# The down-projection's banks evicted one by one, with the activation table, a held product and the tail's sums and multiplies moved

## The chip, the cores and the metric

The kernel runs on one core of one Trainium2 chip. The time of a run is the device time in microseconds (us). Shown are the median of three timed runs of the kernel before, and one further execution that the hardware profiler recorded; all rows of the trace are from that one.

The core has TensorE (PE, matmuls; PEld are its weight loads), VectorE (DVE), ScalarE (ACT), GpSimd (POOL) and SyncE (SP), which issues most of the transfers. SBUF holds the operands, and PSUM holds eight banks of 128 x 512 fp32 into which PE adds.

## The reference, cut to what matters

One layer: a token mixer with a residual, then a gated MLP with a residual, then a last norm. The change is in the last two lines.

```python
h = modulate(rmsnorm(x), sh2, sc2)
up = conv(h @ w_up) + conv_b              # (1024 tokens, 2 * 2816)
a, b = split(up)
x = x + g2 * ((silu(a) * b) @ w_down)     # w_down: 2816 x 1024
return rmsnorm(x) * final_norm            # x * rsqrt(mean(x*x) + eps) * final_norm
```

Everything is fp32: 1024 tokens, 1024 channels, 22 blocks of 128 hidden channels.

## The kernel before

Tensors lie transposed: channels on the 128 partitions, tokens along the row. `hf` is a half of the tokens (512) and `d` one of eight channel tiles; `xs[hf][d]` is a 128 x 512 tile of the residual stream, and the final result.

**The down-projection as seven products.** Hidden blocks, channels and tokens are each cut in two, and the 2 x 2 block product is made from seven products instead of eight, in the order 1, then 2 with 5, then 6 with 3 (interleaved), then 7, then 4 (list `steps`). A product has NJ = 11 steps; a step (p, j) multiplies one 128 x 512 block of activations with a 128 x 512 block of weights into four banks, one for each channel tile. A product of fp32 accuracy is three matmuls of a high and a low part (`mm3`, L107), so a step is 12 matmuls of 512 columns; the high part is a cast on ACT (L801), the low part a subtraction on DVE (L802). Sums and differences of blocks that the seven products need are made by DVE (L812). Products 1, 2, 6, 7 and 4 use one set of four banks and add on top of what stands there; 5 and 3 use another set. Product 4 adds onto product 7, so that PE may write a bank for product 4 only after DVE has read product 7 from it.

**Loads.** `prepare_d(n + 3)` keeps the operands three steps ahead: SP loads blocks (`da`, four buffers; `ra`, `rb`, `rb2` stay), then come the cast and the subtraction. A `da` buffer is reloaded when DVE has split what was in it.

**Evictions.** After the last step of a product, the loop at the end of the kernel treats the four banks: `evac` (L1110, DVE) computes xs = bank * gate + xs; products 1 and 5 are copied to `hold` tiles (ACT, L1212, L1215); product 1's copies are put back into the banks after product 2 is out (L1218); product 5's copies are added into the second half when product 7 ends. `squares` squares an xs tile on ACT (L1134) and adds it into `acc[hf]` on GpSimd (L1142).

**Norm and output.** `finish_first`, called after step (7, 3), sums `acc[0]` over the partitions with a matmul against ones (`ss`), makes rstd = exp(-0.5 * ln(...)) with two ACT instructions (L1146, L1147), and multiplies: `outputs` handles eight channel tiles, two to one store. Seven tiles are one DVE instruction (L1160: xs * gain * rstd), the eighth is ACT (times gain, L1157) and GpSimd (times rstd, L1158). Stores go alternately from SP and from ACT (L1162). The last step (4, 10) is cut in two halves of 256 tokens. `finish_last` sends, behind each half's matmuls, one `ss` matmul of `acc[1]`; at the very end come four more `ss` matmuls per half, one for each new square, and `outputs` again.

**The activation table.** `exp_ln` (L182) orders a table load for Ln and Exp (L184) behind a given ACT instruction: here behind the last Silu of the up-projection (L993).

**What sets the order.** PE runs in the order in which the code is written. The other engines' streams are ordered when the kernel is built, by what each instruction needs and where it stands in the code; each engine then runs its own stream strictly in order and waits on semaphores. GpSimd's last work of the up-projection is the store of a gated block (`gd`, L997), an addition (L1004) and its store (L1005).

## Time and profile before

| what | us |
|---|---|
| median of three timed runs | 1050.42 (1049.86 to 1051.85) |
| the profiled execution's own time | 1047.94 |
| its span | 1046.2 |
| PE busy | 1001.2 |
| DVE busy | 854.6 |
| ACT busy | 549.2 |
| GpSimd busy | 190.5 |

Times in rows are us from the start of the span. A timeline row is: start, duration, engine, line of the kernel, operation, output<-inputs, shape and count; in brackets the idle time of the engine before it and what ended that. Several like instructions in a row are merged, and then the duration runs from the first one's start to the last one's end. A row of the chain of waits is: start, duration, what the end was waiting for at that time. A row of waits is: who waited for whom, total, times, longest. A row of windows is: stretch, its length, then busy time and count of PE, PEld, DVE, ACT and POOL, then the clock granted to PE (1.00 is full), the busy share of the DMA engines and GB/s. PE rows of 512 columns are drawn with an overlap: twelve take 2.72 from start to next start. The letter q (SPq, ACTq) marks an engine's issuing of transfers.

### The profile page before, as it was taken

How to read it: one execution, taken by the hardware profiler on the slowest of the kernel's cores; microseconds unless marked ns; L12 is line 12 of the kernel's file. 1: busy time of each engine (PE TensorE's matmuls, PEld its weight loads, DVE VectorE, ACT ScalarE, POOL GpSimd, SP SyncE). 2: the span in 40 equal slices, each digit the busy share in tenths (PEclk: the TensorE clock that was granted, in tenths of full speed). 3: DMA queues.
4: the chain of work that ended last, by engine and by line, in shares of the span. 5: the costliest groups of instructions: out<-in, count | busy, mean ns of one | idle time of the engine just before them, and what ended most of it. 6: DMA issues, size and time to landing. Idle time of an engine off the chain costs nothing.

```text
span 1046.2 us, 12684 instructions
## 1 busy us (share of the span) xinstructions
PE 1001.2 (96%) x4481; PEld 815.4 (78%) x4481; DVE 854.6 (82%) x1197; ACT 549.2 (52%) x888; POOL 190.5 (18%) x163
## 2 busy tenths in 40 slices
PE   7989999998999989999999999999999999999995
PEld 5768868886777768877888888888888788888874
DVE  7967899689988849999977788777776776988883
ACT  5465585442733547665555455555554544644442
POOL 3437203222141030011100101101001000200210
PEclk8999999999999999999999999999999999999998
DMA  8743232455487442233222222332334787223642
GB/s 315 258 151 111 81 110 83 149 174 182 149 280 262 155 167 81 86 137 129 105 99 91 105 102 107 131 111 101 111 111 151 272 283 240 101 81 111 201 141 81
DMA packets 60817, 154.21 MB, mean 147 GB/s; under 512 B 6641, under 2 KB 9809, under 8 KB 60754
## 3 DMA queue, kind: packets, MB, share of 16 engines
q1 hardware_dynamic: 54192, 134.00, 37.8%
q0 software_dynamic: 4928, 17.30, 4.3%
q10 hardware_dynamic: 1634, 2.10, 0.6%
q8 instruction: 35, 0.57, 0.2%
q14 instruction: 28, 0.23, 0.1%
HBM read 127.69 MB, written 25.69 MB: 147 GB/s over the span
## 4 chain that ended last, share of the span: by engine, by line
PE 62%; DVE 23%; DMA 5%; ACT 4%; issue 4%; POOL 2%; SPq 0%; POOLq 0%; ACTq 0%; DVEq 0%
PE dn L107 18%; PE upy L107 14%; PE upx L107 9%; PE upz L107 9%; PE pp L107 8%; DVE wl L153 3%; DVE ada L219 2%; DMA ada<-in_adaT_dram 2%; DVE xs L802 2%; DVE hl L275 2%; POOL le L347 1%; DVE la L376 1%; DVE ua L812 1%; DVE lq L359 1%; PE ss L107 1%
## 5 line engine op out<-in xcount | busy, mean ns | idle before, releaser
L107 PE MATMUL dn<-xs 128*128 128x512 f32 (+1 forms) x480 | 111.1, 386 | 1.7 <-DVE xs L802 1.3
L107 PE MATMUL dn<-ws 128*128 128x512 f32 x456 | 108.3, 394 | 2.3 <-DVE xs L1110 2.3
L107 PEld LDWEIGHTS dn<-xs 128*128 128x128 f32 x480 | 88.5, 188 | 21.1 <-DVE xs L802 2.1
L107 PEld LDWEIGHTS dn<-ws 128*128 128x128 f32 x456 | 86.7, 190 | 20.9 <-issue 2.7
L107 PE MATMUL upy<-sh,xs 128*128 128x512 f32 x264 | 86.6, 390 | 2.1 <-DVE cb L944 2.1
L107 PE MATMUL upy<-sh,ws 128*128 128x512 f32 x264 | 86.4, 389 | 0.0
L153 DVE TENSOR_TENSOR wl<-raw,wh 128x1024 fp32r<-128x1024 f32 (+1 forms) x50 | 64.2, 1285 | 27.1 <-ACT wh L152 26.8
L997 POOL DMA_DIRECT2D gd<-y x22 | 12.0, 546 | 375.7 <-DVE y L996 358.7
L107 PE MATMUL pp<-hh,wh 128*128 128x512 f32 x176 | 73.7, 419 | 2.7 <-ACT hh L274 1.4
L107 PE MATMUL pp<-hl,wh 128*128 128x512 f32 x176 | 70.8, 402 | 4.8 <-DVE hl L275 4.8
L107 PE MATMUL pp<-hh,wl 128*128 128x512 f32 x176 | 70.8, 402 | 2.6 <-DVE wl L153 2.6
L802 DVE TENSOR_TENSOR xs<-ua,xs 128x512 fp32r<-128x512 f32 x78 | 60.6, 782 | 14.8 <-ACT xs L801 14.8
L802 DVE TENSOR_TENSOR ws<-ua,ws 128x512 fp32r<-128x512 f32 x76 | 55.1, 727 | 15.7 <-ACT ws L801 15.7
L107 PE MATMUL upx<-hh,xs 128*128 128x512 f32 x192 | 62.8, 392 | 2.5 <-DVE x L693 2.5
L801 ACT CAST ws<-ua 128x512 fp32r<-128x512 f32 x76 | 47.0, 622 | 34.4 <-PE upy L107 17.2
L152 ACT CAST wh<-raw 128x1024 fp32r<-128x1024 f32 (+1 forms) x50 | 50.4, 1008 | 26.8 <-DMA raw<-in_w_out_dram 10.8
L801 ACT CAST xs<-ua 128x512 fp32r<-128x512 f32 x78 | 48.1, 622 | 30.5 <-PE upy L107 17.4
L812 DVE TENSOR_TENSOR ua<-ua 128x512 f32<-128x512 f32 x88 | 60.2, 687 | 2.1 <-DMA ua<-in_w_up_dram 0.3
L347 POOL TENSOR_TENSOR le<-b 128x512 f32<-128x512 f32 x24 | 37.1, 1549 | 134.1 <-DVE lq L359 53.8
L107 PE MATMUL upz<-sh,ws 128*128 128x512 f32 x184 | 60.4, 389 | 0.0
L937 DVE SCALAR_TENSOR_TENSOR y<-ca,vec,y 128x1023 f32<-128x1023 f32 (+1 forms) x44 | 56.3, 1280 | 4.3 <-ACT y L934 3.5
L107 PEld LDWEIGHTS upy<-sh,xs 128*128 128x128 f32 x264 | 49.5, 188 | 13.2 <-DVE cb L944 2.9
(261 smaller groups left out, 2521.2 us busy)
## 6 DMA issues: line engine op xcount, KB each, us to landing
ua<-in_w_up_dram SPq DMA_DIRECT2D x49, 512.0 KB, 3.4
ada<-in_adaT_dram SPq DMA_DIRECT2D x32, 512.0 KB, 3.4
gd<-y POOLq DMA_DIRECT2D x22, 512.0 KB, 2.9
raw<-in_w_qkru_dram SPq DMA_DIRECT2D x18, 512.0 KB, 3.3
da<-gd SPq DMA_DIRECT2D x36, 256.0 KB, 2.8
da<-in_w_down_dram SPq DMA_DIRECT2D x36, 256.0 KB, 3.4
raw<-in_w_out_dram SPq DMA_DIRECT2D x16, 512.0 KB, 4.4
x<-in_xT_dram SPq DMA_DIRECT2D x24, 256.0 KB, 4.3
```

The source lines that it names most:

```text
L107: pe.matmul(out=out, lhsT=lhsT, rhs=rhs, start=start, stop=stop, skip_group_check=more)
L152: act.copy(out=wh, in_=raw)
L153: dve.tensor_tensor(out=wl, in0=raw, in1=wh.bitcast(F32), op=ALU.subtract)
L219: dve.scalar_tensor_tensor(out=a, in0=a, scalar=1.0, in1=cb, op0=ALU.mult, op1=ALU.mult, accum_out=acc)
L275: mark["split"] = dve.scalar_tensor_tensor(out=l, in0=t, scalar=sh, in1=h.bitcast(F32), op0=ALU.add, op1=ALU.subtract)
L347: pool_e.tensor_tensor(out=e.rearrange("p (n h) -> p n h", n=nb), in0=b.rearrange("p (n h) -> p n h", n=nb), in1=bb[:, :, 0, h - 1:h].broa ...
L359: dve.tensor_tensor(out=ql.rearrange("p e (n h) -> p e n h", h=h), in0=q2.rearrange("p e (n two h) -> p e n two h", two=2, h=h)[:, :, :, 1 ...
L801: act.copy(out=h, in_=src)
L802: dve.tensor_tensor(out=l, in0=src, in1=h.bitcast(F32), op=ALU.subtract)
L812: eng.tensor_tensor(out=out, in0=a, in1=b, op=ALU.subtract)
L937: dve.scalar_tensor_tensor(out=y[:, sh:], in0=c[:, :S - sh], scalar=cw[j], in1=y[:, sh:], op0=ALU.mult, op1=ALU.add)
L997: nc.gpsimd.dma_start(out=gd[i], in_=ya)
```

## The change

1. `exp_ln` is called behind the last copy of product 1 to `hold`, no longer behind the last Silu.
2. The treatment of the banks moves from the loop into `done`, which is called for bank d right behind that bank's last matmul; `prepare_d(n + 3)` of a product's last step comes after it.
3. Product 5's copies are added (`evac` from `held[5, d]`) in the steps (7, 3) to (7, 6), no longer at product 7's end.
4. The second half's tiles 4 to 7 lie side by side in one tile, `xs_tail`; in the steps (4, 0) to (4, 3) ACT multiplies each of them by its gain, in place.
5. In the last step the squares of tiles 0 to 2 (first 256 tokens) and 0 (last 256) are added into `acc[1]` by GpSimd; `ss` is then two matmuls for the first part and four for the last, all behind the last product's matmuls.
6. In the tail, tiles 4 to 7 are one DVE multiply by rstd (1024 columns) and one store of 512 KB from GpSimd's queue; tiles 0 to 3 stay single multiplies, with stores from SP. In the first half's `outputs` the eighth tile is a DVE instruction like the others.

On ACT, at the end of the up-projection (`y` is the gated block, `ra` and `rb` operands of product 1), before:

```order
L801 CAST xs<-ra 128x512
L993 ACTIVATE y<-y 128x1024
L184 ACT_TABLE_LOAD
L801 CAST xs<-rb 128x512
L801 CAST ws<-ra 128x512
```

and changed, at the end of product 1:

```order
L801 CAST xs<-da 128x512 x4
L801 CAST ws<-da 128x512 x2
L1136 COPY hold<-dn 128x512 x4
L184 ACT_TABLE_LOAD
L801 CAST ws<-da 128x512
L801 CAST ws<-rb 128x512
```

The load has moved behind 19 casts and the four copies of product 1.

On DVE, from the first half's output multiplies to the eviction of product 7 (`o` are output tiles, `da<-da,rb` makes a weight block of product 4), before:

```order
L1160 SCALAR_TENSOR_TENSOR o<-xs_6731,vec,r 128x512
L802 TENSOR_TENSOR xs<-da,xs 128x512
L802 TENSOR_TENSOR xs<-rb_7337,xs 128x512
L812 TENSOR_TENSOR da<-da,rb 128x512
L802 TENSOR_TENSOR xs<-da,xs 128x512
L802 TENSOR_TENSOR xs<-rb_7362,xs 128x512
L802 TENSOR_TENSOR ws<-da,ws 128x512
L802 TENSOR_TENSOR ws<-rb_7405,ws 128x512
L812 TENSOR_TENSOR da<-da,rb 128x512
L802 TENSOR_TENSOR ws<-da,ws 128x512 x2
L812 TENSOR_TENSOR da<-da,rb 128x512 x2
L802 TENSOR_TENSOR xs<-da,xs 128x512 x2
```

and changed:

```order
L1193 SCALAR_TENSOR_TENSOR o<-xs_6728,vec,r 128x512
L802 TENSOR_TENSOR xs<-da,xs 128x512
L802 TENSOR_TENSOR xs<-rb_7334,xs 128x512
L802 TENSOR_TENSOR xs<-da,xs 128x512
L802 TENSOR_TENSOR xs<-rb_7390,xs 128x512
L802 TENSOR_TENSOR ws<-da,ws 128x512
L802 TENSOR_TENSOR ws<-rb_7402,ws 128x512
L812 TENSOR_TENSOR da<-da,rb 128x512 x2
L802 TENSOR_TENSOR ws<-da,ws 128x512 x2
L812 TENSOR_TENSOR da<-da,rb 128x512 x2
L802 TENSOR_TENSOR xs<-da,xs 128x512 x2
```

The first `da<-da,rb` has moved behind four subtractions. In both, one more `da<-da,rb` and one `xs<-da,xs` follow, and then the four evictions of product 7. The additions of product 5's copies stand, in both, some 70 rows further up, among the splits of products 6 and 3.

On ACT in the tail (the `sq` are squares, `r` is rstd), changed:

```order
L1167 ACTIVATE sq<-xs_6719 128x256
L1179 ACTIVATE r<-ss,epsb 128x256
L1167 ACTIVATE sq<-xs_6720 128x256
L1180 ACTIVATE r<-r 128x256
L1179 ACTIVATE r<-ss,epsb 128x256
L1180 ACTIVATE r<-r 128x256
```

Before, all eight squares came first, then Ln, Exp, Ln, Exp. Now the last square of the second 256 tokens stands between the first Ln and its Exp.

```diff
@@ -990,9 +990,7 @@
         else:
             act.copy(out=u["ca"][:, T:], in_=pp)
             ya = conv(u["ca"], i)
-            last = act.activation(out=ya, in_=ya, func=AF.Silu)
-            if i == NFF - 1:
-                exp_ln(last)
+            act.activation(out=ya, in_=ya, func=AF.Silu)
             dve.tensor_tensor(out=ya, in0=ya, in1=u["yb"], op=ALU.mult)
             nc.gpsimd.dma_start(out=gd[i], in_=ya)
             if i < NFF // 2:
@@ -1114,18 +1112,53 @@
     def down_mm(p, j):
         (ah, al), (bh, bl) = split_d.pop((p, j))
         ah, al = flat(ah), flat(al)
+        if p == 7 and 3 <= j < 7:
+            evac(1, j + 1, held[5, j - 3])
+        if p == 4 and j < 4:
+            x = xs[1][4 + j]
+            act.activation(out=x, in_=x, func=AF.Copy, scale=vec[:, V_FN + 4 + j:V_FN + 5 + j])
         if p in (1, 5) and j == 0:
             sets["b" if p == 5 else "a"] = [bank("dn") for _ in range(4)]
         pp = sets["b" if p in (5, 3) else "a"]
         more = p not in (1, 5)
-        cuts = ((0, T // 2), (T // 2, T // 2)) if p == 4 and j == NJ - 1 else ((0, T),)
-        for lo, n in cuts:
+        end = j == NJ - 1
+        for lo, n in ((0, T // 2), (T // 2, T // 2)) if p == 4 and end else ((0, T),):
             for d in range(4):
                 mm3(pp[d][:, lo:lo + n], bh[:, d], bl[:, d], ah[:, lo:lo + n], al[:, lo:lo + n],
-                    not more and j == 0, j == NJ - 1, more)
-            if n < T:
-                finish_last(pp, lo, n)
-        return pp
+                    not more and j == 0, end, more)
+                if end:
+                    done(p, d, pp[d], lo, n)
+
+    held = {}
+
+    def hold(p, d, pp):
+        held[p, d] = dn["o"].tile([P, T], F32, tag="hold", name="hold", bufs=8)
+        return act.copy(out=held[p, d], in_=pp)
+
+    def done(p, d, pp, lo, n):
+        if p == 1:
+            last = hold(1, d, pp)
+            if d == 3:
+                exp_ln(last)
+        elif p == 5:
+            hold(5, d, pp)
+        elif p == 2:
+            evac(0, d, pp)
+            act.copy(out=pp, in_=held[1, d])
+            squares(0, d)
+        elif p == 6:
+            evac(0, 4 + d, pp)
+        elif p == 3:
+            evac(0, 4 + d, pp)
+            squares(0, 4 + d)
+        elif p == 7:
+            evac(1, 4 + d, pp)
+            squares(1, 4 + d)
+        else:
+            sq = acc[d, lo] = square(evac(1, d, pp, lo, n), "sq", n)
+            if d < (1 if lo else 3):
+                a = acc[1][:, lo:lo + n]
+                pool_e.tensor_tensor(out=a, in0=a, in1=sq, op=ALU.add)
 
     acc = {}
 
@@ -1147,37 +1180,39 @@
         act.activation(out=r, in_=r, func=AF.Exp, scale=-0.5)
         return r
 
-    def outputs(hf, lo, n, r):
-        for k in range(0, NK, 2):
-            o = dn["o"].tile([P, 2, T], F32, tag="o", name="o", bufs=4)[:, :, 0:n]
+    def store(q, hf, k, m, lo, n, o):
+        q.dma_start(out=outT[hf, k:k + m, :, lo:lo + n].rearrange("k p t -> p k t"), in_=o)
+
+    def outputs(hf, lo, n, r, k0=0, k1=NK):
+        for k in range(k0, k1, 2):
+            if n == T:
+                o = dn["o"].tile([P, 2, n], F32, tag="o", name="o", bufs=4)
+            else:
+                o = dn["o"].tile([P, 2, n], F32, tag="hold", name="hold", bufs=8)
             for i in range(2):
-                x = xs[hf][k + i][:, lo:lo + n]
-                fn = vec[:, V_FN + k + i:V_FN + k + i + 1]
-                if k + i == NK - 1:
-                    act.activation(out=o[:, i], in_=x, func=AF.Copy, scale=fn)
-                    pool_e.tensor_tensor(out=o[:, i], in0=o[:, i], in1=r, op=ALU.mult)
-                else:
-                    dve.scalar_tensor_tensor(out=o[:, i], in0=x, scalar=fn, in1=r,
-                                             op0=ALU.mult, op1=ALU.mult)
-            (nc.scalar if k % 4 else nc.sync).dma_start(
-                out=outT[hf, k:k + 2, :, lo:lo + n].rearrange("k p t -> p k t"), in_=o)
+                dve.scalar_tensor_tensor(out=o[:, i], in0=xs[hf][k + i][:, lo:lo + n],
+                                         scalar=vec[:, V_FN + k + i:V_FN + k + i + 1], in1=r,
+                                         op0=ALU.mult, op1=ALU.mult)
+            store(nc.scalar if k % 4 and not hf else nc.sync, hf, k, 2, lo, n, o)
 
     def finish_first():
         ss = bank("ss")
         mm(ss, ones, acc[0], True, True)
         outputs(0, 0, T, rstd_out(ss, T))
 
-    def finish_last(pp, lo, n):
-        ss = bank("ss")[:, 0:n]
-        mm(ss, ones, acc[1][:, lo:lo + n], True, False)
-        for d in range(4):
-            acc[d, lo] = square(evac(1, d, pp[d], lo, n), "sq", n)
-
-        def rest():
-            for d in range(4):
-                mm(ss, ones, acc[d, lo], False, d == 3)
-            outputs(1, lo, n, rstd_out(ss, n))
-        acc["rest", lo] = rest
+    def finish_last():
+        n = T // 2
+        for lo, order in ((0, (3, None)), (n, (1, 2, None, 3))):
+            ss = bank("ss")[:, 0:n]
+            for d in order:
+                sq = acc[1][:, lo:lo + n] if d is None else acc[d, lo]
+                mm(ss, ones, sq, d == order[0], d == order[-1])
+            r = rstd_out(ss, n)
+            o = dn["o"].tile([P, 4, n], F32, tag="o", name="o", bufs=4)
+            dve.tensor_tensor(out=o, in0=xs_tail[:, :, lo:lo + n],
+                              in1=r.unsqueeze(1).broadcast_to([P, 4, n]), op=ALU.mult)
+            store(nc.gpsimd, 1, 4, 4, lo, n, o)
+            outputs(1, lo, n, r, 0, 4)
 
     prepare_d(EARLY)
     for n in range(EARLY):
@@ -1189,45 +1224,26 @@
     dn["blk"] = ctx.enter_context(tc.tile_pool(name="blk", bufs=1, reuse_waits="tile"))
     dn["x"] = ctx.enter_context(tc.tile_pool(name="dx", bufs=1, reuse_waits="tile"))
     dn["o"] = ctx.enter_context(tc.tile_pool(name="do", bufs=1, reuse_waits="tile"))
+    xs_tail = dn["x"].tile([P, 4, T], F32, name="xs_tail")
     for hf, d in [(h, d) for h in (1, 0) for d in range(NK)]:
-        xs[hf][d] = dn["x"].tile([P, T], F32, name=f"xs{hf}{d}")
-
-    held = {}
+        xs[hf][d] = (xs_tail[:, d - 4] if hf and d >= 4
+                     else dn["x"].tile([P, T], F32, name=f"xs{hf}{d}"))
+
     x_loads = ([(0, d) for d in range(4)] + [(0, d) for d in range(4, 8)]
                + [(1, d) for d in range(4, 8)] + [(1, d) for d in range(4)])
     for n in range(EARLY, len(steps)):
-        prepare_d(n + 3)
+        p, j = steps[n]
+        if j < NJ - 1:
+            prepare_d(n + 3)
         if n >= 2 * NJ - 2 and n % 2 == 0 and x_loads:
             hf, d = x_loads.pop(0)
             ld(xs[hf][d], x1d[hf][d])
-        p, j = steps[n]
-        pp = down_mm(p, j)
+        down_mm(p, j)
+        if j == NJ - 1:
+            prepare_d(n + 3)
         if (p, j) == (7, 3):
             finish_first()
-        if j < NJ - 1:
-            continue
-        for d in range(4):
-            if p == 1:
-                held[1, d] = dn["o"].tile([P, T], F32, tag="hold", name="hold", bufs=8)
-                act.copy(out=held[1, d], in_=pp[d])
-            elif p == 5:
-                held[5, d] = dn["o"].tile([P, T], F32, tag="hold", name="hold", bufs=8)
-                act.copy(out=held[5, d], in_=pp[d])
-            elif p == 2:
-                evac(0, d, pp[d])
-                act.copy(out=pp[d], in_=held[1, d])
-                squares(0, d)
-            elif p == 6:
-                evac(0, 4 + d, pp[d])
-            elif p == 3:
-                evac(0, 4 + d, pp[d])
-                squares(0, 4 + d)
-            elif p == 7:
-                evac(1, 4 + d, held[5, d])
-                evac(1, 4 + d, pp[d])
-                squares(1, 4 + d)
-    for lo in (0, T // 2):
-        acc["rest", lo]()
+    finish_last()
 
 
 def _tiles(w):
```

## The prediction

> **What bounds the kernel now.** I read the page first, then the waits of TensorE (PE) over the second half, then the chain of waits and the timeline of each place that came out of it.
>
> ```profile
> PE 1001.2 (96%) x4481; PEld 815.4 (78%) x4481; DVE 854.6 (82%) x1197; ACT 549.2 (52%) x888; POOL 190.5 (18%) x163
> ```
> ```profile
> PE dn L107 <- DVE xs L1110: 2.3, 1, 2.3
> PE dn L107 <- DVE xs L802: 1.3, 1, 1.3
> PE dn L107 <- ACT xs L801: 0.4, 1, 0.4
> ```
>
> PE is busy 96% of the span, and the change takes next to no matmul away. So it can win only where PE stands still, and in the tail after PE's last product. From 640 us on there are just three standstills, all in the down-projection. The first place, from the chain of waits around 825 us, and the DVE and POOL timelines there:
>
> ```profile
> 823.21 1.28 ACT L184
> 824.51 0.63 ACT xs L801
> 825.16 2.01 DVE xs L802
> 827.21 22.98 PE dn L107 x100
> ```
> ```profile
> 823.23 1.22 DVE L996 TENSOR_TENSOR y<-y 128x1024 f32<-128x1024 f32 x1 [0.26 <-ACT y L993]
> 825.31 1.29 POOL L1004 TENSOR_TENSOR s<-s,y 128x512 f32<-128x512 f32 x1
> ...
> 785.84 0.68 DVE L802 TENSOR_TENSOR ws<-ua,ws 128x512 fp32r<-128x512 f32 x1
> 786.77 1.30 POOL L1004 TENSOR_TENSOR s<-s,y 128x512 f32<-128x512 f32 x1
> ```
>
> The table load (L184) stands between the last Silu and a cast that PE needs. The cast comes 1.3 us late, DVE's subtraction (L802) then falls onto the GpSimd addition and takes 2.0 instead of 0.68 us, and PE loses 0.4 + 1.3. The second place, from the chain and the timelines around 980 to 1000 us:
>
> ```profile
> 979.16 5.76 DVE L1160 SCALAR_TENSOR_TENSOR o<-xs,vec,r 128x512 f32<-128x512 f32 x7 [0.48 <-ACT r L1147]
> 982.48 1.78 DVE L1160 SCALAR_TENSOR_TENSOR o<-xs,vec,r 128x512 f32<-128x512 f32 x1
> 982.19 1.51 POOL L1158 TENSOR_TENSOR o<-o,r 128x512 f32<-128x512 f32 x1 [9.79 <-ACT o L1157]
> ```
> ```profile
> 986.12 0.57 DVE da L812
> ...
> 988.92 6.04 DMA da<-in_w_down_dram
> ...
> 998.15 0.67 DVE xs L1110
> ```
> ```profile
> 998.96 4.58 PE L107 MATMUL dn<-ws 128*128 128x512 f32 x12 [2.33 <-DVE xs L1110]
> ```
>
> The output multiplies of the first half (L1160) hold DVE. What stands behind them frees the `da` buffers late, their reloads land late, and DVE, in order, reaches the eviction of product 7 (L1110) at 998.15. Product 4 adds into the same banks, so PE waits 2.33. It then pays again: these twelve matmuls take 4.58 us where the twelve ahead took 2.88, for the granted clock fell to 0.50 in the window from 1000 to 1002 us:
>
> ```profile
> 993.75 2.88 PE L107 MATMUL dn<-ws 128*128 128x512 f32 x12
> ...
> 1000.00:1002.00 2.00, 2.00 (x6) 1.54 (x6) 2.00 (x3) 2.00 (x4) 1.32 (x2) 0.50 0.01 3
> ```
>
> The third place is the tail:
>
> ```profile
> 1028.94 1.59 ACT L1134 ACTIVATE sq<-xs 128x256 f32<-128x256 f32 x4 [7.85 <-DVE xs L1110]
> 1031.59 3.62 PE L107 MATMUL ss<-sq,ones 128*128 128x256 f32 x16
> 1033.52 0.47 ACT L1146 ACTIVATE r<-ss,epsb 128x256 f32<-128x256 f32 x1 [1.06 <-PE ss L107]
> 1034.02 0.42 ACT L1147 ACTIVATE r<-r 128x256 f32<-128x256 f32 x1
> 1034.47 2.86 DVE L1160 SCALAR_TENSOR_TENSOR o<-xs,vec,r 128x256 f32<-128x256 f32 x7 [2.53 <-ACT r L1147]
> 1040.99 0.72 POOL L1158 TENSOR_TENSOR o<-o,r 128x256 f32<-128x256 f32 x1 [3.07 <-DVE o L1160]
> 1041.74 0.38 ACTq L1162 DMA_DIRECT2D out_dram<-o  x1
> ```
> ```profile
> GB/s 0 0 0 0 0 0 0 0 0 0 0 0 0 0 48 342 301 347 316 347 183 320 357 335 352 323 352 349 46 65 354 198 0 0 0 0 0 0 0 0
> DMA packets 2176, 2.10 MB, mean 123 GB/s; under 512 B 128, under 2 KB 2176, under 8 KB 2176
> ```
>
> That last view covers 1030 to 1047 in slices of 0.425 us: the output flows from 1036.0 at some 340 GB/s, pauses at 1041.9 for the last pair, which waits for ScalarE and then GpSimd, and ends at 1043.6, 2.6 us before the span does.
>
> **The change, part by part.** *Table load moved: 1.68 us.* The cast can start where the load does now, at 823.21, and ends at 823.84; DVE's subtraction follows its multiply (823.23 + 1.22) at 824.46 and ends at 825.14, before the GpSimd addition at 825.31. That is the order of the rows at 785.84 and 786.77, from an earlier round of the same loop, where it took 0.68. PE's third matmul of that step, which needs it, is due at about 825.25. Both standstills go (0.38 + 1.30). The other end is 0: if the subtraction is still caught by the addition, it ends as now. I take the full value, since the row at 785.84 is the same neighbourhood. The load goes behind the copies of product 1:
>
> ```profile
> 844.47 2.26 ACT L1212 COPY hold<-dn 128x512 f32<-128x512 f32 x4
> 848.87 1.14 ACT L801 CAST xs<-da 128x512 fp32r<-128x512 f32 x2 [1.10 <-PE dn L107]
> ```
>
> Two casts follow it there, and then ACT idles 1.10 until PE frees the next operand's buffer. Operands are made up to three steps ahead, so its 1.28 is hidden by that idle time and the next; uncovered it would cost 1.28. The Trainium skill (ScalarE: Activation LUTs, "What ACT_TABLE_LOAD costs") adds about 1.38 us of drain to a load of 1283 ns. The load agrees; the next cast stood 0.02 behind it, so no drain shows after it, and the sum is the same by either.
>
> *First half's last multiply onto DVE: 0.7 us off the stall, and perhaps the clock.* Seven multiplies took 5.76 because one met the GpSimd multiply and took 1.78; the other six share 3.98, 0.66 each. Eight without GpSimd take 5.3: 0.4 us earlier, although DVE does more. The first subtraction `da<-da,rb` (0.57, the row at 986.12) also moves behind the splits that free buffers, so the last reload ahead of the eviction, whose transfer now runs 6.04 us from 988.92, can start about 0.95 earlier. It is slow because the output stores run beside it (a GpSimd store of twice its size has 2.9, below), so its landing follows by between 0.3 and 0.95; I take 0.7. The stall becomes 1.6. Does the clock still fall? The trace has a longer stall without a fall, 2.5 us between 386 and 390 (the waits of that stretch, and the window that holds its end, with 12 matmuls in 2.73):
>
> ```profile
> PE upx L107 <- DVE x L693: 2.5, 1, 2.5
> 388.00:392.00 4.00, 2.73 (x12) 2.25 (x13) 4.00 (x5) 1.23 (x2) 3.20 (x2) 1.00 0.35 131
> ```
>
> So I count the 1.7 us (4.58 less 2.88) as saved; the other end is 0.
>
> *The rest before the tail: 0.* The orders above show DVE's evictions and the held product's addition where they already stood. The four scaled copies (0.57 each, as the `hold` copies, 2.26 / 4) go onto ScalarE, whose casts there wait 1.56 for PE at each step:
>
> ```profile
> 1003.63 1.14 ACT L801 CAST ws<-da 128x512 fp32r<-128x512 f32 x2 [1.56 <-issue]
> ```
>
> Without that cover they cost up to 2.3.
>
> *Tail: 1.4 us.* On the clock of the old rows: the first square ends at 1029.35; three GpSimd additions of 0.72 (the row at 1040.99) bring the sum to 1031.65; its matmul (3.62 / 8 = 0.45) to 1032.1; Ln to 1032.6; a square of the other half, 0.42, now queued between; Exp to 1033.45 instead of 1034.44. The four-channel multiply is priced by L996, 1.22 for 1024 columns; four single ones follow at 0.41. That gives 1034.7 and 1036.3 for the first half. The second half's rstd is ready at 1034.8 (four sums matmuls, Ln, Exp), so DVE goes on to 1037.5 and 1039.15. The last store is issued 2.5 us earlier than 1041.74. But the 2.10 MB still flow at 340 GB/s, 6.2 us, and start no earlier: GpSimd's store, 1034.7 plus its issue, brings data at about 1035.9.
>
> ```profile
> L997 POOL DMA_DIRECT2D gd<-y x22 | 12.0, 546 | 375.7 <-DVE y L996 358.7
> gd<-y POOLq DMA_DIRECT2D x22, 512.0 KB, 2.9
> ```
>
> So data ends at 1042.1 to 1042.3 instead of 1043.6. I take 1.4; the ends are 2.5 (the issue decides) and 0. The Trainium skill (DMA: Bandwidth & Descriptors, the table at its head) gives a GpSimd-issued transfer about 1 us to the first byte against 0.6 from SyncE and ScalarE. That speaks against this store; by it the tail would save an estimated 1.0. No run here shows the first byte; the 2.9 from issue to landing is all that the trace has.
>
> **Sum.** 1.68 + 0.7 + 1.7 + 1.4 = 5.5 us. The profiled execution took 1047.94 (span 1046.2 and 1.7 around it), so 1042.4 for its like. It lies 2.5 under the median of the runs, 1050.42; from that median: **1044.9**.
>
> **Rivals.** *The clock falls all the same* (0.20): the 1.6 us stall is still a stall, and 2.33 fell where 2.5 did not, so length alone does not decide. Saving 3.8: 1046.6. *More comes* (0.10): the stall shrinks by 1.0 and the store's issue decides in the tail (2.5), 6.9: 1043.5.
>
> *Transfers hide it* (0.16): the reloads behind the stall land when the engines have moved the bytes, whenever issued, and the tail likewise. For it: the 6.04 us of a 256 KB load. Against it: the stores that slow it also move up. Only the table's 1.68 stays: 1048.7.
>
> *GpSimd's stores held, slower* (0.07): while DVE multiplies, GpSimd can't write the lists for its two stores. Both then start at DVE's end, 1039.2, at 4 x 0.55 each for four rows per partition instead of one, 1043.6, and land up to 6.7 later:
>
> ```profile
> gd<-y POOLq DMA_DIRECT2D x1, 512.0 KB, 6.7
> ```
>
> With the 2.1 from landing to the end, 1052.4, against 1046.2; less the 4.1 gained earlier, 2.1 slower: 1052.5. It decides once the last GpSimd store lands more than 4.1 us after 1044.1. The Trainium skill describes such a lock (SBUF — State Buffer, "Who interferes with whom") for copies, not for multiplies of two tensors. By it this would not happen, and the trace agrees: L997's issue at 786.22 to 786.76 overlapped a DVE subtraction and took the usual 0.54.
>
> ```profile
> 786.22 0.54 POOL L997 DMA_DIRECT2D gd<-y  x1 [16.32 <-DVE y L996]
> ```
>
> **How the numbers follow.** The forecast has 0.47. A measurement here can tell about 0.2%, 2.1 us, from no change. Faster by more: 0.47 + 0.20 + 0.10 = 0.77; within: 0.16; slower: 0.07. The forecast's own range is 1043.5 to 1046.6, with the clock's and the tail's bounds; 1043.0 to 1048.9 takes in the case of the hidden transfers and leaves out some 0.15.
>
> **What would show it.** Right: no wait of PE near 825; the table load behind the `hold` copies with no PE wait after it; eight multiplies in about 5.3; a PE wait at the start of product 4 of 1.3 to 2.0 with the clock at 1.00 behind it; the last store issued 2 us or more sooner after PE's last product, and a tail without a gap in the DMA row. Wrong: a subtraction of 2 us still at 825; reloads landing at the same distance from PE as now; a clock of 0.5 behind product 4; a last landing that is GpSimd's.

## The result and the profile after

The changed kernel takes 1046.01 us (median of 10 runs, 1042.62 to 1047.99) where the kernel before, run beside it, takes 1050.72 (10 runs, 1048.32 to 1056.59). The ratio is 0.995 with an interval of 0.9934 to 0.9965: 4.7 us faster. The forecast was 1044.9, 5.5 us under the median shown before.

The profiled executions are compared stretch by stretch. Up to about 823 us both kernels issue the same work, and still their profiles (and those of the experiments) start one and the same `dn` step ahead of that place anywhere between 810.7 and 818.2 us. One reason is falls of the clock granted to PE at places that no edit touches: the four profiles without a fall between 200 and 800 us start that step at 810.7 to 812.7, the eight with two or more at 813.5 to 818.2. So I use two lengths: from the start of that step to the start of PE's last group of product 4 ("the stretch"), and from there to the end of the span ("the tail"). Before: 810.83 to 1025.15 to 1046.2, that is 214.32 and 21.05. After: 813.51 to 1023.91 to 1043.9, that is 210.40 and 19.99. The stretch gave 3.92, the tail 1.06, together 4.98; the timed difference is 4.7 (interval 3.7 to 6.9).

Of the changed kernel's page, the head and the engines:

```profile
span 1043.9 us, 12663 instructions
...
PE 1002.6 (96%) x4473; PEld 815.6 (78%) x4473; DVE 853.7 (82%) x1194; ACT 550.7 (53%) x889; POOL 192.8 (18%) x166
```

PE's share is still 96%. What moved shows in PE's waits from 640 us on (engine, tile and line waited for; total, times, longest):

```profile
PE dn L107 <- DVE xs_tail L1108: 1.6, 1, 1.6
PE ss L107 <- POOL acc L1161: 0.6, 1, 0.6
PE dn L107 <- DVE xs L802: 0.4, 1, 0.4
```

Where 2.3 + 1.3 + 0.4 stood, 1.6 + 0.4 are left in the stretch; the 0.6 lies in the tail, where PE has no more product to do.

**At 825 us.** The changed kernel's chain of waits, and its DVE and POOL timelines there:

```profile
825.33 1.06 ACT y L993
827.56 0.69 DVE xs L802
828.30 21.86 PE dn L107 x95
```
```profile
826.42 1.23 DVE L994 TENSOR_TENSOR y<-y 128x1024 f32<-128x1024 f32 x1 [0.27 <-ACT y L993]
827.56 0.68 DVE L802 TENSOR_TENSOR xs<-rb,xs 128x512 fp32r<-128x512 f32 x1
828.16 2.21 DVE L802 TENSOR_TENSOR ws<-ra,ws 128x512 fp32r<-128x512 f32 x1
828.50 1.31 POOL L1002 TENSOR_TENSOR s<-s,y 128x512 f32<-128x512 f32 x1
```

No table load stands in the chain any more. The subtraction that PE needs takes 0.68 and is done before the GpSimd addition; PE waits 0.37 for it. The next subtraction, for the other operand, meets that addition and takes 2.21; PE has no wait for it.

**At 980 to 1000 us.** DVE's and PE's rows, the reload in the chain, and the clock in the window behind the stall:

```profile
980.24 5.39 DVE L1193 SCALAR_TENSOR_TENSOR o<-xs,vec,r 128x512 f32<-128x512 f32 x8 [0.48 <-ACT r L1180]
977.61 1.02 PE L107 MATMUL ss<-acc,ones 128*128 128x512 f32 x2
999.33 2.98 PE L107 MATMUL dn<-ws 128*128 128x512 f32 x12 [1.62 <-DVE xs_tail L1108]
```
```profile
989.07 6.33 DMA da<-in_w_down_dram
998.52 0.67 DVE xs_tail L1108
999.33 27.83 PE dn L107 x123
```
```profile
1000.00:1002.00 2.00, 2.00 (x11) 1.66 (x10) 2.00 (x4) 2.00 (x4) 0.79 (x1) 1.00 0.05 19
```

Eight multiplies take 5.39 where seven took 5.76. The stall is 1.62, and the twelve matmuls behind it take 2.98 at a clock of 1.00.

**The tail.** The changed kernel's timeline from PE's last group on:

```profile
1023.91 5.75 PE L107 MATMUL dn<-xs 128*128 128x512 f32 x36
1030.74 0.70 PE L107 MATMUL ss<-acc,ones 128*128 128x256 f32 x2 [0.63 <-POOL acc L1161]
1031.48 0.47 ACT L1179 ACTIVATE r<-ss,epsb 128x256 f32<-128x256 f32 x1 [0.95 <-PE ss L107]
1032.60 1.23 DVE L1212 TENSOR_TENSOR o<-xs_tail,r 128x1024 f32<-128x1024 f32 x1 [2.18 <-ACT r L1180]
1034.12 0.78 POOL L1184 DMA_DIRECT2D out_dram<-o  x1 [2.75 <-DVE o L1212]
1034.64 3.88 SPq L1184 DMA_DIRECT2D out_dram<-hold  x4
1036.46 1.67 DVE L1193 SCALAR_TENSOR_TENSOR hold<-xs,vec,r 128x256 f32<-128x256 f32 x4
```

DVE's last multiply ends 14.2 us behind the start of the group (1036.46 + 1.67), and the last store is issued by 1038.52 (1034.64 + 3.88), 14.6 behind it. Before, it was 17.0 (1041.74 + 0.38). Yet the tail is only 1.06 shorter. The output's flow tells why; here from 1034 to 1047 in slices of 0.325 us, first of the kernel before, then of the changed one:

```profile
GB/s 0 0 0 0 0 0 0 299 337 296 353 296 350 347 151 321 318 356 321 362 350 321 350 350 167 0 107 347 331 22 0 0 0 0 0 0 0 0 0 0
```
```profile
GB/s 0 0 0 0 189 359 318 353 353 309 303 347 312 334 227 340 356 359 337 328 287 350 343 315 35 0 0 0 0 0 0 0 0 0 0 0 0 0 0 0
```

Counted from the start of PE's last group, the flow began at 11.2 and ended at 18.3; now it begins at 11.5 and ends at 17.9. The pause before the last pair is gone, but the flow starts 0.3 later. From the last byte to the end of the span it was 2.75 us and is 2.1; what fills that time no row shows.

### The profile page after: what moved, and what is told of

It reads as the page before. It is cut to its first block, busy times and chain, and to the rows that moved or that the text cites. A ratio compares the mean times of both kernels' runs of the same rounds, so it can differ in the third digit from the quotient of the medians.

```text
span 1043.9 us, 12663 instructions
## 1 busy us (share of the span) xinstructions
PE 1002.6 (96%) x4473; PEld 815.6 (78%) x4473; DVE 853.7 (82%) x1194; ACT 550.7 (53%) x889; POOL 192.8 (18%) x166
## 3 DMA queue, kind: packets, MB, share of 16 engines
q10 hardware_dynamic: 546, 1.05, 0.3%
## 4 chain that ended last, share of the span: by engine, by line
PE 67%; DVE 20%; ACT 4%; DMA 3%; issue 3%; POOL 2%; SPq 0%; DVEq 0%; POOLq 0%; ACTq 0%
PE dn L107 17%; PE upy L107 14%; PE pp L107 13%; PE upx L107 9%; PE upz L107 9%; DVE wl L153 3%; PE sc L107 2%; DVE ada L219 1%; DVE xs L802 1%; DVE hl L275 1%; DVE ua L812 1%; POOL le L347 1%; DMA raw<-in_w_out_dram 1%; DVE la L376 1%; DVE ws L802 1%
## 5 line engine op out<-in xcount | busy, mean ns | idle before, releaser
L153 DVE TENSOR_TENSOR wl<-raw,wh 128x1024 fp32r<-128x1024 f32 (+1 forms) x50 | 66.4, 1328 | 27.4 <-ACT wh L152 27.1
L801 ACT CAST xs<-ua 128x512 fp32r<-128x512 f32 x78 | 48.1, 622 | 30.5 <-PE upy L107 17.4
```

Source lines behind the costliest of these rows:

```text
L153: dve.tensor_tensor(out=wl, in0=raw, in1=wh.bitcast(F32), op=ALU.subtract)
L801: act.copy(out=h, in_=src)
```

## The experiments

The theory after this reading: the gain has four sources, the table load (1.6), the stall at product 4 (0.7), the clock behind it (1.6 in this pair of profiles) and the tail (1.1). The rivals: that one of them is not caused by its edit, the clock above all, or that the two parts priced at nothing carry some of it. Every ratio is against the kernel before, run beside it on the same chip. An interval is some 3 to 4.5 us wide, so a source of 1 us shows in the trace's stretches only.

### Each part alone

**Table load alone.** The kernel before, with only the load moved:

```diff
-            last = act.activation(out=ya, in_=ya, func=AF.Silu)
-            if i == NFF - 1:
-                exp_ln(last)
+            act.activation(out=ya, in_=ya, func=AF.Silu)
...
-                act.copy(out=held[1, d], in_=pp[d])
+                last = act.copy(out=held[1, d], in_=pp[d])
+                if d == 3:
+                    exp_ln(last)
```

> The kernel before with one part of the change alone: the table load behind the last copy of product 1 instead of behind the last Silu. My theory (the load delays one cast and pushes one subtraction onto the GpSimd addition): no PE wait of 0.3 us or more between 820 and 832 us, a subtraction of 0.7 instead of 2.0 us there, and the time 1.6 us lower; the stall at product 4 stays 2.3 us. Rival (the slack is given back at a later wait, as the stall at product 4 hangs on transfers): same PE rows near 825, but the stall at product 4 grows by as much, time unchanged.

Measured: 1049.35 (12 runs) against 1051.4 (35 runs), ratio 0.9975 (0.9959 to 0.999), faster. The stretch is 210.34, the tail 21.03. Its DVE row at the old place of the waits, and PE's at product 4:

```profile
830.18 0.68 DVE L802 TENSOR_TENSOR xs<-rb,xs 128x512 fp32r<-128x512 f32 x1
1002.49 2.98 PE L107 MATMUL dn<-ws 128*128 128x512 f32 x12 [2.07 <-DVE xs L1108]
```

Both waits at 825 are gone, by the load alone. From the start of the stretch to the `ss` matmul of the first half it is 163.60 (816.73 to 980.33) where it was 165.70 (810.83 to 976.53); this 2.10 belongs to the edit. It is more than the two waits' 1.68, because the rows of waits do not hold all that PE lost there: the two steps around them took 7.92 before, from their start to the start of the next (821.71 to 829.63), and take 5.74 here (827.61 to 833.35). The stall at product 4, which this edit does not touch, is 2.07 here, and no clock fell behind it. So the stretch of this one profile is 4.0 shorter, of which some 1.9 belongs to the execution and not to the edit.

**Eighth tile alone.** The kernel before, with the first half's last channel multiplied on DVE like the others:

```diff
-                if k + i == NK - 1:
+                if k + i == NK - 1 and hf:
```

> The kernel before with one part alone: the eighth tile of the first half's output is a DVE multiply like the other seven, without ScalarE and GpSimd. My theory (one multiply collided with GpSimd): the eight take 5.3 to 5.4 us instead of 5.76 for seven, the stall at product 4 falls from 2.3 to 1.6 us, the clock stays at 1.00 behind it, and the time is 0.7 to 2.3 us lower. Rival (the eighth instruction lengthens DVE's queue): the eight take 6.4, the stall grows to 3 us, the time is 0.7 us or more higher. Rival (reloads land when the engines have moved the bytes): multiplies shorter, stall 2.2 to 2.4 as before, time unchanged.

Measured: 1049.92 against 1051.4, ratio 0.9989 (0.9969 to 1.0009): by time alone not to be told from no change. The trace tells:

```profile
984.05 5.39 DVE L1160 SCALAR_TENSOR_TENSOR o<-xs,vec,r 128x512 f32<-128x512 f32 x8 [0.48 <-ACT r L1147]
1003.30 2.97 PE L107 MATMUL dn<-ws 128*128 128x512 f32 x12 [1.78 <-DVE xs L1110]
```

One tile more on DVE, and DVE is done 0.37 sooner; the stall is 1.78. The wait at 825 (1.4) stays, the tail is 21.04. The edit does two things at once: it shortens the multiplies, and it alone already moves the first `da<-da,rb` behind the splits, as in the changed kernel. Together they start the last slow reload ahead of the eviction 11.5 us behind the first half's `ss` matmul instead of 12.4. What each of the two is worth was not told apart.

**Tail alone.** The changed kernel with the table load and the first half's eighth tile put back as they were (the two edits above, backwards).

> The changed kernel with the table load put back behind the last Silu and the eighth tile of the first half put back on ScalarE and GpSimd, so that the tail's parts are what is left of the change. Theory: the wait at 825 and a stall of about 2.3 at product 4 come back; the tail from the start of the last step to the end of the span is 1.1 us shorter than before, and the time is 1.1 us lower than before. Rival (the tail is a matter of the clock and of the run): no difference from before within 0.5 us.

Measured: 1051.3 against 1051.4, ratio 1.0002 (0.9985 to 1.002), unclear. The tail is 19.94, 1.1 shorter than before, as in the changed kernel; the timed runs can't show 1.1. The stretch is 214.43, as before, but not for the same reasons. PE's rows and windows of 4 us show it:

```profile
827.29 3.87 PE L107 MATMUL dn<-xs 128*128 128x512 f32 x10 [1.30 <-DVE xs L802]
1000.57 3.00 PE L107 MATMUL dn<-ws 128*128 128x512 f32 x12 [2.30 <-DVE xs_tail L1110]
```
```profile
828.00:832.00 4.00, 4.00 (x13) 3.09 (x12) 3.00 (x6) 1.13 (x3) 0.00 (x0) 0.57 1.04 407
```

Here the stall of 2.30 at product 4 was followed by no fall of the clock, although in the kernel before 2.33 was. The fall came at the other place instead, behind the waits of 0.6 and 1.3 at 825: ten matmuls took 3.87 where the kernel before did the same ten, behind waits of 0.4 and 1.3 at the same place, in 2.58:

```profile
825.18 0.73 PE L107 MATMUL dn<-xs 128*128 128x512 f32 x2 [0.38 <-ACT xs L801]
827.21 2.58 PE L107 MATMUL dn<-xs 128*128 128x512 f32 x10 [1.30 <-DVE xs L802]
```

So either of the two old standstills can cost a fall, and which of them does changes from one execution to the next. A place that no edit touches shows the same: at about 390 us PE waits 2.48 to 2.49 for DVE (L693) in all thirteen profiles of this case, and the clock falls behind it in seven of them and not in six. In the kernel before it did not fall; in the changed kernel's profile it did:

```profile
390.50 0.50 PE L107 MATMUL upx<-hh,xs 128*128 128x512 f32 x1 [2.48 <-DVE x L693]
393.00:395.00 2.00, 2.00 (x6) 1.60 (x5) 2.00 (x4) 0.04 (x1) 0.00 (x0) 0.50 0.00 0
```

### What a longer stall costs

The changed kernel, with two more reads of the first bank on DVE ahead of product 7's eviction; they write scratch tiles that nobody reads:

```diff
         elif p == 7:
+            if d == 0:
+                for _ in range(2):
+                    t = dn["o"].tile([P, T], F32, tag="sq", name="sq", bufs=8)
+                    dve.scalar_tensor_tensor(out=t, in0=pp, scalar=modv[:, 44:45],
+                                             in1=xs[1][4], op0=ALU.mult, op1=ALU.add)
             evac(1, 4 + d, pp)
```

> The changed kernel with two more DVE instructions (each reads bank 0 and tile 4 and writes a scratch tile that nobody reads, about 0.7 us) ahead of the eviction of product 7. If a long enough stall is what lowers the clock: the stall grows from 1.6 to about 3.0 us, the windows behind it show a clock near 0.5 for some 3 us, and the time is 1.4 + 1.7 = 3.1 us over the changed kernel. If the clock's fall has to do with the moment and not with the length: the clock stays 1.00 and the time is 1.4 us over the changed kernel.

Measured: 1049.9 against 1051.4, ratio 0.9983 (0.9968 to 0.9999): 3.9 over the changed kernel's median, or 3.5 by the two ratios, as the two were not run side by side. PE's row, and a window behind the stall:

```profile
1001.27 4.31 PE L107 MATMUL dn<-ws 128*128 128x512 f32 x12 [3.33 <-ACT sq L1172]
```
```profile
1004.00:1006.00 2.00, 2.00 (x6) 1.52 (x5) 2.00 (x2) 0.44 (x2) 1.92 (x2) 0.50 0.57 174
```

The stall grew by 1.71: the eviction starts 1.05 later behind the first half's `ss` matmul, and the row says that PE then waited for a square on ScalarE. The twelve matmuls grew by 1.33 (4.31 less 2.98), and the stretch by 3.22 (213.62), the rest lying behind the twelve, while the clock is still down. Here a standstill of PE was paid almost twice, as the clock fell. The same profile has a fall behind a shorter standstill, far ahead of the stretch:

```profile
277.77 0.50 PE L107 MATMUL pp<-yh,wh 128*128 128x512 f32 x1 [1.89 <-ACT us L515]
280.00:282.00 2.00, 2.00 (x6) 1.60 (x5) 2.00 (x4) 2.00 (x4) 0.00 (x0) 0.50 0.26 61
```

### Taking the stall's cause away

The changed kernel, with the first half's output called after three steps of product 4 instead of after four steps of product 7:

```diff
-        if (p, j) == (7, 3):
+        if (p, j) == (4, 2):
             finish_first()
```

> The changed kernel with the norm, multiplies and stores of the first half called after step (4, 2) instead of (7, 3), so that the 2 MB of stores no longer run beside the reloads ahead of the eviction of product 7. If the stall at product 4 hangs on DVE's queue and the transfers behind those multiplies: the wait at product 4 falls from 1.6 to under 0.5 us, no new PE wait over 0.5 us in product 4, time 1.2 to 1.6 us under the changed kernel. If it hangs on something else (PE's own release of operand buffers, the eviction's place behind other DVE work): the wait stays 1 us or more. If the multiplies only move the harm: a new PE wait of 1 us or more inside product 4, time as in the changed kernel.

Measured: 1044.95 (6 runs) against 1051.03 (11 runs), ratio 0.9927 (0.991 to 0.9944). All of PE's waits from 800 us on, and the moved multiplies:

```profile
PE ss L107 <- POOL acc L1161: 0.6, 1, 0.6
PE dn L107 <- DVE ws L802: 0.4, 1, 0.4
```
```profile
1014.10 5.38 DVE L1193 SCALAR_TENSOR_TENSOR o<-xs,vec,r 128x512 f32<-128x512 f32 x8
```

The stall is gone and the stretch is 208.58, 1.82 under the changed kernel; by time the intervals of the two ratios overlap. The 0.4 lies at 911.9 us, ahead of the work that was moved, and the 0.6 in the tail. So the stall came from the first half's output work ahead of product 7's eviction. At the new place the multiplies take as long, and PE waits for nothing behind them. Whether it is DVE's 5.39 or the stores beside the reload that counts for more was not told apart.

### The tail, piece by piece

Three variants of the changed kernel, each with one edit in the tail. Their times (1043.24, 1048.21 and 1047.67) are one run each, so I read the tails. These are steady: where nothing in it was edited, the changed kernel's tail is 19.92 to 19.99 in five profiles, and the old tail 21.03 to 21.05 in three.

**Stores of the four-channel products from ScalarE.**

```diff
-            store(nc.gpsimd, 1, 4, 4, lo, n, o)
+            store(nc.scalar, 1, 4, 4, lo, n, o)
```

> The changed kernel with the two 512 KB stores of the tail issued by ScalarE instead of GpSimd. Theory (GpSimd's path costs a longer start): first output data 0.3 to 0.6 us earlier after the last step's start, and the end as much earlier, since the flow of 2.10 MB sets the end. Rival (only the bytes count): the same tail, 20.0 us from the last step's start to the end of the span, within 0.2.

Measured: a tail of 18.83 instead of 19.99. Its rows, and the flow from 1028 to 1046 in slices of 0.45 us:

```profile
1022.67 5.75 PE L107 MATMUL dn<-xs 128*128 128x512 f32 x36
...
1031.36 1.22 DVE L1212 TENSOR_TENSOR o<-xs_tail,r 128x1024 f32<-128x1024 f32 x1 [2.19 <-ACT r L1180]
1032.62 3.10 ACTq L1184 DMA_DIRECT2D out_dram<-o  x2
```
```profile
GB/s 0 0 0 0 0 0 0 0 0 0 0 0 216 348 335 341 346 326 339 339 341 348 326 360 339 335 23 0 0 0 0 0 0 0 0 0 0 0 0 0
```

From the end of the multiply (1032.58) to the first byte (1033.6) it takes 1.0 us; from GpSimd it took 1.6 (1033.83 to 1035.45). Counted from the start of the issue it is about 0.95 (1032.62) against 1.3 (1034.12); the rest is that GpSimd began to issue 0.29 behind the multiply and ScalarE 0.04. The flow is also steadier. Issue to landing is 3.2 us instead of 4.1. GpSimd's queue thus cost 1.16 us of the kernel's end, twice what had been expected.

**Sums of squares on PE again.** The four GpSimd additions are left out and five matmuls sum the squares for each half:

```diff
-            if d < (1 if lo else 3):
-                a = acc[1][:, lo:lo + n]
-                pool_e.tensor_tensor(out=a, in0=a, in1=sq, op=ALU.add)
...
-        for lo, order in ((0, (3, None)), (n, (1, 2, None, 3))):
+        for lo, order in ((0, (None, 0, 1, 2, 3)), (n, (None, 0, 1, 2, 3))):
```

> The changed kernel without GpSimd's additions in the tail: each half's sum is five matmuls, all behind the last product. Theory: the first Ln starts after five sums matmuls, 2.3 us after the last product's end, against 1.8 now; the tail is 0.4 to 0.6 us longer. Rival (the sums' place does not matter, since bytes set the end): the same tail within 0.2.

Measured: a tail of 20.17, 0.2 longer than with the GpSimd sums, which is the rival's figure and not the 0.4 to 0.6 of the theory. Ahead of the tail, where this edit changes nothing, PE waited 1.2 and 2.25, and the clock fell behind the second:

```profile
989.26 6.89 DMA da<-in_w_down_dram
...
1000.08 4.52 PE L107 MATMUL dn<-ws 128*128 128x512 f32 x12 [2.25 <-DVE xs_tail L1108]
...
1026.23 5.75 PE L107 MATMUL dn<-xs 128*128 128x512 f32 x36
...
1034.18 0.48 ACT L1176 ACTIVATE r<-ss,epsb 128x256 f32<-128x256 f32 x1 [0.94 <-PE ss L107]
```

Ln starts 7.95 behind the group (1034.18 less 1026.23) against 7.57 with the GpSimd sums (1031.48 less 1023.91). So the additions save 0.4 there, of which half reaches the end. And this program, whose five engines do the same work in the same order as the changed kernel's up to the tail, has a stall of 2.25 with a fall where that has 1.62 and none. The reload ahead of the eviction took 6.89 here and 6.33 there. The clock's cost is not abolished.

**Single multiplies ahead of the four-channel one.**

```diff
             r = rstd_out(ss, n)
+            outputs(1, lo, n, r, 0, 4)
             o = dn["o"].tile([P, 4, n], F32, tag="o", name="o", bufs=4)
...
             store(nc.gpsimd, 1, 4, 4, lo, n, o)
-            outputs(1, lo, n, r, 0, 4)
```

> The changed kernel with the four single multiplies and their two 256 KB stores ahead of the four-channel multiply in each half of the tail. If the end is set by when the flow of 2.10 MB begins: the first data come 0.5 us or more earlier and the end follows. If it is set by the last multiply and its store: DVE's end is the same, but the last store is now 512 KB from GpSimd instead of 256 KB from SyncE, and the end is 0.5 to 1.5 us later.

Measured: a tail of 21.14, 1.15 longer, as in the second case. The flow, 1028 to 1046 in slices of 0.45 us:

```profile
GB/s 0 0 0 0 0 0 0 0 0 0 0 0 0 0 0 0 282 307 346 230 0 0 360 350 323 355 303 348 284 316 355 328 173 0 0 0 0 0 0 0
```

The small stores leave early from SyncE (first byte 10.5 us behind the start of PE's last group, against 11.5), are through before GpSimd's large one has begun, and the flow stands still for 0.9 us. The tail loses all that the change had gained there (21.05 before). What counts is not only when the flow starts but that the next store is ready before it runs dry.

### The two parts priced at nothing

The changed kernel with the eviction of each bank put back behind the whole step, and the held product's addition put back into the last step of product 7:

```diff
-        if p == 7 and 3 <= j < 7:
-            evac(1, j + 1, held[5, j - 3])
...
-                if end:
+                if end and p == 4:
                     done(p, d, pp[d], lo, n)
...
+        if j == NJ - 1 and p != 4:
+            for d in range(4):
+                if p == 7:
+                    evac(1, 4 + d, held[5, d])
+                done(p, d, pp[d], 0, T)
```

> The changed kernel with two parts undone: the banks are treated in a loop after a product's last step, and product 5's copies are added at product 7's end. The built instruction streams of all five engines are the same as in the changed kernel, so every theory expects the same time; what differs from the changed kernel's 1046.0 us is what these runs cannot tell from no change, and the wait at product 4 is a further sample of that stall (1.6 us in the changed kernel's profile).

Measured: 1045.14 (6 runs) against 1051.55 (11 runs), ratio 0.9932 (0.9911 to 0.9953); stall 1.64, stretch 210.79, tail 19.92. All five engines' instructions stand in the same order as in the changed kernel. The rewriting of these two parts in the source moves nothing.

### Two versions that go further

The late first half and ScalarE's stores together; and the same with the four-channel multiply cut into two of two channels, each with its own store of 256 KB:

```diff
+            for k in (4, 6):
+                o = dn["o"].tile([P, 2, n], F32, tag="o", name="o", bufs=4)
+                dve.tensor_tensor(out=o, in0=xs_tail[:, k - 4:k - 2, lo:lo + n],
+                                  in1=r.unsqueeze(1).broadcast_to([P, 2, n]), op=ALU.mult)
+                store(nc.scalar, 1, k, 2, lo, n, o)
```

> The changed kernel with both edits that helped: the first half's norm and output after step (4, 2), and the tail's 512 KB stores from ScalarE. If the two gains are independent: no PE wait over 0.5 us at product 4, a tail of 18.8 us from the last step to the end, and a time 2.5 to 3 us under the changed kernel's 1046.0, near 1043.5. If the first half's stores, now 10 us nearer to the tail, disturb it: a tail over 19.5 us.

> As the run before, with the four-channel multiply and its 512 KB store cut into two of two channels and 256 KB each. If the end is set by the moment at which the 2.10 MB begin to flow: the first data come 0.5 us earlier and the tail is 18.3 us. If more instructions and issues on the path cost what the earlier start gains: the tail stays at 18.8 or grows.

Measured: 1042.5 (ratio 0.9905, 0.9884 to 0.9927) and 1042.02 (0.9908, 0.9887 to 0.9929), 6 runs each, against 1051.55. Stretches 207.95 and 208.24, tails 18.74 and 18.12. PE waits nowhere in the stretch of the first; of the second, the tail:

```profile
1022.38 5.75 PE L107 MATMUL dn<-xs 128*128 128x512 f32 x36
...
1031.06 1.29 DVE L1213 TENSOR_TENSOR o<-xs_tail,r 128x512 f32<-128x512 f32 x2 [2.19 <-ACT r L1180]
1031.79 0.98 ACTq L1184 DMA_DIRECT2D out_dram<-o  x2
```

Both beat the kernel before by some 9 us, twice the gain of the change. The pairs' first store leaves after half the multiply, which shortens the tail by another 0.6; by time the two can't be told apart.

## Why the prediction was right, and where it was off

- **Table load, 1.68.** Measured 1.60: from the start of that `dn` step to the `ss` matmul of the first half the changed kernel gained 1.60 (810.83 and 976.53 before, 813.51 and 977.61 after). The mechanism was right: the subtraction came ahead of the GpSimd addition and took 0.68, and the copies of product 1 hid the load; it alone removed both waits. The size is near, but not as worked out: with no wait left, as in the run with the load alone, it is 2.10, and in the changed kernel's profile a wait of 0.37 was left. Not foreseen was that the next subtraction would then meet the addition.
- **Eighth multiply, 0.7 off the stall.** Measured 0.71 in this pair (2.33 to 1.62); eight multiplies took 5.39 where 5.3 was said. The reload landed 0.64 nearer to the `ss` matmul (18.43 to 17.79), inside the 0.3 to 0.95. But the pair flatters it. In the three profiles with the eighth tile on ScalarE and GpSimd the stall is 2.33, 2.07 and 2.30; in the six with it on DVE and the first half's output at the same place it is 1.62, 1.78, 1.90, 2.25, 1.63 and 1.64. The means are 2.23 and 1.80, a gain of 0.43. The size of the 0.71 is partly luck.
- **Clock, 1.7.** Measured 1.60 in this pair of profiles (4.58 to 2.98). That it came out so is in part luck, and the reason given does not hold. The prediction took the stall of 2.5 at 390 us that had no fall as a sign that 1.6 would have none; the same stall had a fall in seven of the thirteen profiles. At product 4 the clock fell behind 2.33, 2.25 and 3.33 and not behind 2.30, 2.07, 1.90 or anything shorter; elsewhere it fell behind 1.89 and behind 0.6 + 1.3. So length alone does not decide around 2 us. With the old stall it fell in one profile of three, with the shorter one in one of six: too few to say what the edits save on average. The kernel before has two places where it can fall in the stretch, the changed one has one, shorter. So the 1.7 is no fixed part of the gain. The Trainium skill (TensorE: Matmul & The Clock Gate, "Part 1: The HAM clock gate") calls the window of about 3.4 us in which activity is watched free-running. That agrees with falls that move from place to place; that a whole window must be idle does not agree, since PE stood only 1.89 to 2.33 in three of them.
- **Zero for the rest before the tail.** Right. With the banks' treatment and the held product's addition put back, all five engines' instructions keep their order, so these two parts can bring nothing. The four scaled copies are in the changed kernel; PE has no wait in product 4 behind the stall at its start.
- **Tail, 1.4.** This is the term that was mis-sized; it measured 1.06. "GpSimd's store, 1034.7 plus its issue, brings data at about 1035.9" put the first byte at 10.75 behind the group; it came at 11.5. The multiply ended 0.37 later than worked out: GpSimd's sum reached PE 0.33 later and its two matmuls take 0.70, not 0.45, of which ScalarE's rows won back a part. The issue began 0.3 behind the multiply; and from its end to the first byte it took another 0.55. The last byte came 0.4 sooner than before, not 1.4. The other 0.65 was gained between the last byte and the end of the span, which the prediction had left unchanged. The prediction's sentence on the Trainium skill (DMA: Bandwidth & Descriptors, the table at its head) had the tail at 1.0. That is nearer than the rows, but by luck, as the last byte moved by 0.4 only. With ScalarE's store the first byte comes about 0.4 sooner behind the start of the issue, which agrees with the page's difference; the kernel's end moved by 1.16.
- **The sum.** 5.5 was said; the stretches give 1.60 + 0.71 + 1.60 + 1.06 = 4.97, the times 4.7. That these agree is luck in part: the clock's 1.60 and some of the 0.71 belong to this pair of executions, and the timed interval, 3.7 to 6.9, is too wide to test the terms.
- **The rivals.** *The clock falls all the same* did not happen at 1.6 to 1.9 in five profiles, but did happen to a sister program at 2.25. *More comes* did not: the stall shrank by 0.71 and the tail by 1.06. *Transfers hide it* did not come as a whole, for the stall shrank and the gain is 3.7 or more by the interval, not 1.7; but a part of it is true. In the seven profiles with the edit the reload starts 11.45 to 11.54 behind the `ss` matmul, against 12.39 in the three without; it lands at 17.4 to 18.4, against 18.2 to 18.4. So between all and almost nothing of the 0.9 us comes through. *GpSimd's stores held* fell: the second was issued in 0.76 us while DVE multiplied (1036.84 and 1036.46), and they landed 4.1 after their issue. The Trainium skill (SBUF — State Buffer, "Who interferes with whom") makes its exception for `tensor_tensor`; beside both issues DVE ran SCALAR_TENSOR_TENSOR, which that section does not name.

## What to carry to other kernels

An operation that a second engine shares with DVE can make DVE slower than doing all of it alone; before dividing a group of small operations, compare the mean of the undisturbed ones with the one that met the other engine. For the end of a kernel whose output flows at a steady rate, work out the first byte, the supply behind it and the last byte separately: issuing the last store 2.4 us sooner brought 0.4, while changing the queue that issues the first one brought 1.2. And do not book a fall of the clock seen in one profile as a sure gain of an edit: count the standstills that can cause one, and remove the standstill at its source.

## What the runs showed of the hardware

- **The granted clock** falls to 0.50 for some 3 us behind standstills of PE as short as 1.89 us, in some executions and not in others: behind one and the same standstill of 2.48 us in seven profiles of thirteen. It also fell behind two waits of 0.6 and 1.3 with two matmuls between. Each of the four falls measured in the stretch cost 1.3 to 1.6 us over the next ten or twelve matmuls.
- **DVE beside GpSimd.** A subtraction with both inputs in SBUF takes 0.68 alone and 2.0 to 2.2 beside a GpSimd addition of 1.3.
- **A 512 KB store** of 1 KB rows has its first byte 1.6 us behind the end of the multiply from GpSimd and 1.0 from ScalarE, and lands 4.1 and 3.2 after its issue.
- **Open:** why the reload ahead of product 7's eviction varies (6.33 in one profile, 6.89 in another) so that the same stall is 1.62 and 2.25, and what fills the 1.6 to 2.75 us between the last byte of output and the end of the span.
